# A table of 1,326 steps written anew: the order and the engine of every step of a thresholded attention on one core

## The chip, the cores and the metric

The kernel runs on one core of a Trainium2 chip. The metric is the device time of one execution in microseconds (us), lower is better. Three runs of the kernel before gave 174.76, 174.87 and 173.38 us, with a median of 174.76 us.

## The reference

There are 8 x 12 = 96 heads, each with 512 queries and 512 keys of 64 numbers. The weights are a softmax, those not above the threshold of 0.1 are set to zero, what is left is normalized again, and the values are summed with it:

```python
scores = np.einsum('bhqd,bhkd->bhqk', Q, K) * scale
weights = np.exp(scores - np.max(scores, axis=-1, keepdims=True))
weights = weights / (np.sum(weights, axis=-1, keepdims=True) + 1e-10)
weights = np.where(weights > threshold, weights, 0)
weights = weights / (np.sum(weights, axis=-1, keepdims=True) + 1e-10)
return np.einsum('bhqk,bhkd->bhqd', weights, V).astype(np.float32)
```

With 512 random keys very few queries have a weight above 0.1. The kernel finds these few rows and fills the rest of the output with zeros.

## The kernel before, in words

Two heads make a pair (48 of them) and two pairs a quad (24). For each quad, numbered 0 to 23, the steps are these, named as in the plan. SP issues the loads of queries and keys (step `q`, line 334, 512 KB; step `k`, line 330, four transfers of 128 KB). `qcast` (lines 367, 369, 371) turns queries to half precision on ACT, DVE or GpSimd (POOL in the profile). `ktr` (L381) and `qtr` (L410) transpose keys and queries on TensorE (PE), `kev` (L389 on ACT, L391 on DVE) and `qev` (L416) copy the results to SBUF, and `kh` (L396, L398, L400) casts the keys. `sc` (L438) makes the scores of 128 keys for both heads of a pair, `ex` their approximate exponentials (L447 on ACT, L449 on DVE; 384 instructions, two for each `sc`), and `sm` (L468) adds them up on PE into one PSUM bank for a whole group of pairs. `bits` (L425 on GpSimd, L427 on ACT, L429 on DVE) and `norms` (L478) make squared norms for a check that closes the kernel. `z` (L607, SP) fills the output of a quad with zeros, 512 KB each.

The pairs form three groups of 24, 16 and 8. When the last `sm` of a group is done, `y`, `d`, `fl`, `mx` (L486 or L488, L495, L500, L504) find its candidates. They are worked on in six stages x = 0 to 5, three for the first group, two for the second, one for the third. A stage is a chain: `m`, `ix`, `qi` and `qf` (L513, L519, L524, L529) make row numbers; `gq` (L534) gathers query rows with an indirect transfer issued by GpSimd; `xm` and `xev` (L541; L547 on ACT, L549 on DVE) transpose them; `xqk` (L556, PE) makes exact scores; `xexp` (L562, ACT), `xcut` and `xkeep` (L566, L570, DVE) keep what is above the threshold; `vi` and `oi` (L575, L580) turn it into row numbers; `gv` (L585) gathers the value rows and `scatter` (L600) writes them to the output, both indirect transfers issued by GpSimd. So GpSimd issues 18 indirect transfers, and `scatter` of a stage waits for the landing of its `gv`. At the end `nm` and four `check` steps (L491, L750 to L763) feed a branch (L772 to L784) that is not taken.

All loads, keys, casts and squares share 32 buffers of one ring called big; the transposed keys of a quad stay in it until the `xqk` of its stage has read them. A load waits until the step that had the buffer before is done.

No scheduler runs when the kernel is built. `ORDER` (L13) is a string of 1,326 words, a step number in base 36 and a letter for the engine (P PE, V DVE, A ACT, G GpSimd, S the SP queue, Q the queue of ACT, N none). `Plan.order` walks through it, takes buffers and emits the step; each engine works its own steps in that order, one after the other:

```python
        for i, e in seq:
            name, engs, _, deps, _, fn, takes, gives, _ = self.ops[i]
            assert e in engs and all(self.ids[d] in done for d in deps), name
            for pool, key in takes:
                self.held[pool, key] = idle[pool].pop(0)
            fn(e)
            for pool, key in gives:
                idle[pool].append(self.held[pool, key])
            done.add(i)
```

Only steps with more than one engine in their list can change engine: `qcast`, `kev`, `kh`, `ex`, `bits`, `y` and `xev`, and the loads of quad 0, which may go by SP or by ACT's queue. The loads of quads 0 and 1 are cut into halves of 128 KB (keys of one head) and 256 KB (queries of one pair); these are the first twelve transfers.

Of the kernel before, what the change touches and what calls it, by code (L numbers as in the profile page):

```python
# [853 lines left out]
```

## Time and profile before

| | kernel before |
|---|---|
| median of three runs | 174.76 us |
| the profiled execution | 173.97 us |
| its span in the trace | 172.1 us |
| busy: PE, DVE, ACT, GpSimd | 159.3, 150.6, 146.7, 133.7 us |
| exponentials on ACT and on DVE | 238 and 146 |
| zero fills, key loads, query loads by SP | 24, 95, 26 transfers |

The table says that four engines are busy for most of the span, so it does not tell what bounds the time. The rows are read for three stretches: the ramp (to 16 us), the steady part (16 to 149.5 us, where the last exponential ends), and the tail, where the last group's chain runs.

### The profile page before, as it was taken

How to read it: one execution, taken by the hardware profiler on the slowest of the kernel's cores; microseconds unless marked ns; L12 is line 12 of the kernel's file. 1: busy time of each engine (PE TensorE's matmuls, PEld its weight loads, DVE VectorE, ACT ScalarE, POOL GpSimd, SP SyncE). 2: the span in 40 equal slices, each digit the busy share in tenths (PEclk: the TensorE clock that was granted, in tenths of full speed). 3: DMA queues.
4: the chain of work that ended last, by engine and by line, in shares of the span. 5: the costliest groups of instructions: out<-in, count | busy, mean ns of one | idle time of the engine just before them, and what ended most of it. 6: DMA issues, size and time to landing. Idle time of an engine off the chain costs nothing.

```text
span 172.1 us, 5805 instructions
## 1 busy us (share of the span) xinstructions
PE 159.3 (93%) x2190; PEld 62.5 (36%) x2190; DVE 150.6 (88%) x353; ACT 146.7 (85%) x294; POOL 133.7 (78%) x201
## 2 busy tenths in 40 slices
PE   5699999999999999999989999989999999999940
PEld 1253544342444234334432443434324333432410
DVE  5398999899999989989999899999999999989630
ACT  2279999999999999999899999999999999746300
POOL 5049794999988979993796999999899985226762
PEclk9999999999999999999999999999999999999996
DMA  4999998959899999878999996999999980000000
GB/s 103 290 281 175 268 255 224 265 132 313 183 244 304 277 229 339 242 181 251 276 280 289 221 272 156 365 409 311 318 304 338 415 344 13 2 3 8 3 3 9
DMA packets 67453, 38.27 MB, mean 222 GB/s; under 512 B 51941, under 2 KB 64349, under 8 KB 67424
## 3 DMA queue, kind: packets, MB, share of 16 engines
...
q0 software_dynamic: 576, 0.13, 0.5%
q10 hardware_dynamic: 528, 0.13, 0.3%
...
## 4 chain that ended last, share of the span: by engine, by line
PE 55%; DMA 15%; DVE 10%; POOL 6%; ACT 4%; issue 4%; SPq 2%; POOLq 0%; DVEq 0%
PE one L438 20%; PE sum L468 19%; DMA qs<-in_Q_dram,idx 7%; PE one L556 6%; PE one L381 4%; PE one L410 3%; ACT e L447 3%; DMA out_dram<-zero 3%; POOL big L425 2%; DMA big<-in_K_dram 2%; DVE e L449 2%; DMA big<-in_Q_dram 2%; POOL qh L371 2%; PE one L541 2%; SPq L330 2%
## 5 line engine op out<-in xcount | busy, mean ns | idle before, releaser
L447 ACT ACTIVATE e<-one 128x512 f16<-128x512 f32 x238 | 123.3, 638 | 3.0 <-PE one L438 2.5
L449 DVE TENSOR_SCALAR e<-one 128x512 uint16<-128x512 f32 x146 | 93.5, 682 | 4.2 <-PE one L438 3.4
L438 PE MATMUL one<-big 64*128 64x512 f16 x384 | 66.4, 385 | 0.3
L468 PE MATMUL sum<-e,w_s 128*32 128x512 f16 (+1 forms) x768 | 58.4, 385 | 0.3 <-DVE y L495 0.2
L425 POOL TENSOR_TENSOR big<-big 128x512 bf16<-128x512 f16 x56 | 56.9, 1037 | 0.0
L400 POOL CAST big<-big 128x512 f16<-128x512 f32 x46 | 27.6, 611 | 8.6 <-DVE big L429 3.3
L371 POOL CAST qh<-big 128x512 f16<-128x512 f32 x45 | 26.5, 612 | 7.9 <-DVE qh L369 6.3
L438 PEld LDWEIGHTS <-big 64*128 64x128 f16 x384 | 17.1, 95 | 36.5 <-issue 28.0
L468 PEld LDWEIGHTS <-w_s 128*32 128x32 f16 (+1 forms) x768 | 15.3, 95 | 31.6 <-issue 27.0
L389 ACT COPY big<-one 128x512 f32<-128x512 f32 (+1 forms) x33 | 18.5, 591 | 3.8 <-PE one L381 3.8
L416 DVE COPY big<-one 128x512 f16<-128x512 f16 (+1 forms) x52 | 19.2, 396 | 1.2 <-PE one L410 0.7
L381 PE MATMUL one<-identity_f,big 64*128 64x64 f32 x384 | 18.1, 231 | 1.6 <-DMA big<-in_K_dram 1.4
L381 PEld LDWEIGHTS one<-identity_f,big 64*128 64x128 f32 x384 | 16.5, 143 | 6.4 <-issue 2.7
L534 POOL DMA_INDIRECT qs<-in_Q_dram,idx x6 | 6.4, 1072 | 12.5 <-DVE idx L524 12.2
L391 DVE COPY big<-one 128x512 f32<-128x512 f32 (+1 forms) x19 | 12.5, 657 | 1.3 <-PE one L381 0.6
L556 PE MATMUL one<-big,xq 128*32 128x512 f32 x96 | 11.5, 598 | 0.4 <-DVE xq L549 0.2
L410 PE MATMUL one<-identity_h,qh 64*128 64x64 f16 x384 | 10.8, 193 | 0.7 <-DVE qh L369 0.4
L410 PEld LDWEIGHTS <-qh 64*128 64x128 f16 x384 | 8.7, 96 | 7.2 <-issue 3.1
L600 POOL DMA_INDIRECT out_dram<-vr,idx x6 | 6.4, 1065 | 2.6 <-issue 1.1
L585 POOL DMA_INDIRECT vr<-in_V_dram,idx x6 | 6.4, 1060 | 2.3 <-DVE cut L566 1.2
L562 ACT ACTIVATE one<-one 128x512 f32<-128x512 f32 x6 | 3.5, 584 | 5.4 <-PE one L556 5.3
L429 DVE TENSOR_SCALAR big<-big 128x512 int32<-128x512 int32 x15 | 7.3, 491 | 0.1
...
## 6 DMA issues: line engine op xcount, KB each, us to landing
...
qs<-in_Q_dram,idx POOLq DMA_INDIRECT x6, 3.4
vr<-in_V_dram,idx POOLq DMA_INDIRECT x6, 2.4
out_dram<-vr,idx POOLq DMA_INDIRECT x6, 2.2
```

Source lines behind the costliest of these rows:

```text
L371: behind(nc.gpsimd.tensor_copy(dst, src))
L381: nc.tensor.matmul(dst[i][:, c:c + D], lhsT=src[ps, n0 + n, r, :], rhs=identity_f32[ps, ps], is_transpose=True, start=True, stop=True)
L389: nc.scalar.copy(dst, src)
L400: behind(nc.gpsimd.tensor_copy(dst, src))
L410: nc.tensor.matmul(dst[i][:, c:c + D], lhsT=src[ps, n0 + n, r, :], rhs=identity_h[ps, ps], is_transpose=True, start=True, stop=True)
L416: nc.vector.tensor_copy(qk_b[big("qk", q)][:, 0, n0:n0 + k, i * SO * D:(i + 1) * SO * D], src)
L425: behind(nc.gpsimd.tensor_tensor(out=dst[:, n, :], in0=src[:, n, :], in1=src[:, n, :], op=ALU.mult))
L438: nc.tensor.matmul(one[at("one", ("sc", hp, t, h))][:], lhsT=qk[ps, 1, n, t * P:(t + 1) * P], rhs=qk[ps, 0, n, :], start=True, stop=True)
L447: nc.scalar.activation(dst, src, ACTF.Exp, scale=scale, bias=-11.0 * math.log(2.0))
L449: nc.vector.tensor_scalar(dst.bitcast(u16), src, scale * LOG2E * 1024.0, 4096.0, op0=ALU.mult, op1=ALU.add)
L468: nc.tensor.matmul(dst[32 * j:32 * j + 32, :], lhsT=w, rhs=x, start=first, stop=False, skip_group_check=True)
L556: nc.tensor.matmul(one[at("one", ("xs", x))][sl, :], lhsT=xq_b[at("xq", x)][:, n, sl], rhs=kt_b[big("kt", quads[j])][:, n, :], start=(n == ...
```

## The change

Only the string is changed. The steps, their instructions and the six stages are the same.

```diff
@@ -10,7 +10,7 @@
-ORDER = """6N fS 1G gS 7P hS 8P 5V 18S 24S 9P 22S aP 23S bP 16S 17Q 2vS iV jP 2tS nP kV lA cP mA
...
+ORDER = """6N fS gQ 1G hS 18Q 7P 24S 22S 8P 3G 5V 23S 16Q 9P 17S aP jP 2tS bP kA lV 2uS iG mA 2vS
...
```

Steps that change engine, as counts of the two tables: `ex` on ACT 238 before, 232 now, on DVE 146 and 152; `kev` on ACT 33 and 35, on DVE 19 and 17 (those of whole quads on ACT 27 and 31, those of halves 6 and 4); `bits` on ACT 5 and 10, on DVE 15 and 11, on GpSimd 28 and 27; `kh` on ACT 1 and 2; `qcast` on DVE 3 and 0, on ACT 0 and 1, on GpSimd 45 and 47; `y` on ACT 1 and 2.

The end of GpSimd's work, in the order in which it stands, before. The index tile tells the stage: idx_174 to idx_179 are stages 0 to 5.

```order
L534 DMA qs_183<-in_Q_dram,idx_177 128x64
L534 DMA qs_184<-in_Q_dram,idx_178 128x64
L534 DMA qs_185<-in_Q_dram,idx_179 128x64
L600 DMA out_dram<-vr_196,idx_176 49152x64
L585 DMA vr_197<-in_V_dram,idx_177 128x64
L600 DMA out_dram<-vr_195,idx_175 49152x64
L600 DMA out_dram<-vr_197,idx_177 49152x64
L585 DMA vr_198<-in_V_dram,idx_178 128x64
L585 DMA vr_199<-in_V_dram,idx_179 128x64
L600 DMA out_dram<-vr_198,idx_178 49152x64
L600 DMA out_dram<-vr_199,idx_179 49152x64
```

And now, from the last squares (L425) on:

```order
L425 TENSOR_TENSOR big_137<-big_133 128x512 x4
L600 DMA out_dram<-vr_194,idx_175 49152x64
L534 DMA qs_183<-in_Q_dram,idx_177 128x64
L600 DMA out_dram<-vr_196,idx_176 49152x64
L534 DMA qs_184<-in_Q_dram,idx_178 128x64
L534 DMA qs_185<-in_Q_dram,idx_179 128x64
L585 DMA vr_197<-in_V_dram,idx_177 128x64
L600 DMA out_dram<-vr_197,idx_177 49152x64
L585 DMA vr_198<-in_V_dram,idx_178 128x64
L585 DMA vr_199<-in_V_dram,idx_179 128x64
L600 DMA out_dram<-vr_198,idx_178 49152x64
L600 DMA out_dram<-vr_199,idx_179 49152x64
```

The stores of stages 1 and 2 (idx_175, idx_176) stood among the transfers of the last three stages; now the one stands ahead of all three `gq` and the other behind the first of them. The `gv` of stages 4 and 5 now follow the store of stage 3 as before, with one store fewer ahead of that.

The end of ACT's work before, from the last exponential on. The cut tiles cut_191 to cut_193 are stages 3 to 5.

```order
L447 ACTIVATE e_150<-one_106 128x512
L486 ACTIVATE y_162<-sum_113,small 64x512
L547 COPY xq_187<-one_108 128x256
L562 ACTIVATE one_110,cut_191<-one_110 128x512
L427 ACTIVATE big_130<-big_122 128x1024
L427 ACTIVATE big_129<-big_127 128x1024
L562 ACTIVATE one_111,cut_192<-one_111 128x512
L547 COPY xq_187<-one_108 128x256
L562 ACTIVATE one_112,cut_193<-one_112 128x512
L427 ACTIVATE big_144<-big_125 128x1024
```

And now, from `y` on:

```order
L486 ACTIVATE y_162<-sum_113,small 64x512
L547 COPY xq_187<-one_109 128x256
L562 ACTIVATE one_111,cut_191<-one_111 128x512
L547 COPY xq_186<-one_107 128x256
L427 ACTIVATE big_133<-big_134 128x1024
L427 ACTIVATE big_125<-big_142 128x1024
L427 ACTIVATE big_133<-big_134 128x1024
L562 ACTIVATE one_109,cut_192<-one_109 128x512
L427 ACTIVATE big_122<-big_120 128x1024
L562 ACTIVATE one_111,cut_193<-one_111 128x512
L427 ACTIVATE big_119<-big_141 128x1024
L427 ACTIVATE big_122<-big_120 128x1024
```

Six squares (L427) stand behind `y` now, against three: three between the copy of stage 4 (L547, xq_186) and its exponential (cut_192), one between that and the exponential of stage 5 (cut_193), two at the end. A seventh, not in these rows, stands just ahead of `y` and behind the last exponential of the steady part; three more stand earlier, against two. The copy of stage 5 has moved from ACT to DVE, that of stage 4 from DVE to ACT.

The first loads in SP's queue before. big_114 and big_115 hold keys and queries of quad 0, big_117 and big_116 those of quad 1, big_120 is the query load of quad 2.

```order
L330 DMA big_114<-in_K_dram 128x4x64 x2
L334 DMA big_115<-in_Q_dram 128x2x256 x2
L334 DMA big_116<-in_Q_dram 128x2x256
L330 DMA big_117<-in_K_dram 128x4x64 x2
L330 DMA big_114<-in_K_dram 128x4x64
L334 DMA big_116<-in_Q_dram 128x2x256
L330 DMA big_117<-in_K_dram 128x4x64 x2
L334 DMA big_120<-in_Q_dram 128x4x256
```

And now:

```order
L330 DMA big_114<-in_K_dram 128x4x64
L334 DMA big_115<-in_Q_dram 128x2x256
L334 DMA big_116<-in_Q_dram 128x2x256
L330 DMA big_117<-in_K_dram 128x4x64 x2
L330 DMA big_114<-in_K_dram 128x4x64
L330 DMA big_117<-in_K_dram 128x4x64 x2
L334 DMA big_116<-in_Q_dram 128x2x256
L334 DMA big_120<-in_Q_dram 128x4x256
```

SP issues one half of the first keys and then the first queries. The other half of the first keys now goes out on ACT's queue at the same time, and behind it on that queue the other queries and one more key half of quad 0 (before, ACT's queue had one key half of the second pair only).

The loads of later quads change places as well. The one the prediction speaks of is the key load of quad 17. Before, its buffer came from a `qcast` step, and 43 exponentials stand in the table between the load and `ktr` of that quad. Now its buffer is that of the keys released by `xqk` of stage 0, and 14 stand between.

## Rows read from the trace of the kernel before

**Rows 1.** Windows of two stretches: us, busy of each engine, granted clock, DMA share, GB/s.

```profile
6.00:16.00 10.00, 9.31 (x106) 4.28 (x106) 7.91 (x21) 7.60 (x17) 5.01 (x11) 1.00 1.11 253
16.00:149.50 133.50, 131.74 (x1908) 51.80 (x1912) 127.65 (x248) 131.48 (x265) 115.67 (x171) 1.00 0.91 259
```

**Rows 2.** Instruction groups by shape: count, busy us, mean ns, idle before.

```profile
L447 ACT ACTIVATE e<-one 128x512 f16<-128x512 f32 x238 | 123.3, 638 | 3.0 <-PE one L438 2.5
...
L371 POOL CAST qh<-big 128x512 f16<-128x512 f32 x45 | 26.5, 612 | 7.9 <-DVE qh L369 6.3 <-DVE y L500 0.7 <-DMA big<-in_Q_dram 0.6
...
L389 ACT COPY big<-one 128x512 f32<-128x512 f32 x27 | 16.4, 637 | 0.0
...
L427 ACT ACTIVATE big<-big 128x1024 bf16<-128x1024 f16 x5 | 5.2, 1053 | 0.0
...
L369 DVE CAST qh<-big 128x512 f16<-128x512 f32 x3 | 1.3, 420 | 2.3 <-DMA big<-in_Q_dram 2.3
...
L396 ACT CAST big<-big 128x512 f16<-128x512 f32 x1 | 0.6, 617 | 0.4 <-DVE big L391 0.4
```

**Rows 3.** Chain that ended last, 158 us to the end: start, us, what.

```profile
162.33 0.21 DVE idx L575
...
163.00 2.42 DMA vr<-in_V_dram,idx
```

**Rows 4.** Timeline of GpSimd, 148 to 170 us: start, us, instruction, idle before.

```profile
148.24 1.07 POOL L534 DMA_INDIRECT qs<-in_Q_dram,idx  x1 [3.75 <-DVE idx L524]
151.31 0.99 POOL L534 DMA_INDIRECT qs<-in_Q_dram,idx  x1 [2.01 <-DVE idx L524]
...
159.84 1.28 POOL L600 DMA_INDIRECT out_dram<-vr,idx  x1 [0.31 <-issue]
161.69 1.01 POOL L600 DMA_INDIRECT out_dram<-vr,idx  x1 [0.57 <-DVE cut L566]
163.00 1.05 POOL L585 DMA_INDIRECT vr<-in_V_dram,idx  x1 [0.30 <-DVE ix L529]
164.36 1.02 POOL L585 DMA_INDIRECT vr<-in_V_dram,idx  x1 [0.31 <-issue]
166.26 1.01 POOL L600 DMA_INDIRECT out_dram<-vr,idx  x1 [0.88 <-DVE okm L763]
167.62 1.00 POOL L600 DMA_INDIRECT out_dram<-vr,idx  x1 [0.35 <-issue]
```

**Rows 5.** Timeline of ACT, 148 to 162.5 us.

```profile
150.51 0.68 ACT L486 ACTIVATE y<-sum,small 64x512 f32<-64x512 f32 x1 [1.02 <-PE sum L468]
...
154.41 1.99 ACT L427 ACTIVATE big<-big 128x1024 bf16<-128x1024 f16 x2
157.41 0.58 ACT L562 ACTIVATE one<-one 128x512 f32<-128x512 f32 x1 [1.01 <-PE one L556]
...
160.56 0.58 ACT L562 ACTIVATE one<-one 128x512 f32<-128x512 f32 x1 [2.04 <-PE one L556]
```

**Rows 6.** Chain that ended last, first 8 us.

```profile
1.47 0.88 SPq L330
...
2.40 3.50 DMA big<-in_Q_dram
```

**Rows 7.** Timeline of ACT, first 9 us.

```profile
6.03 0.37 ACT L389 COPY big<-one 128x256 f32<-128x256 f32 x1 [3.32 <-PE one L381]
```

**Rows 8.** Line 330 (key loads), issues of 0.7 to 1.45 us.

```profile
DMA to landing us min/median/max: 2.8/3.0/3.3
```

**Rows 9.** Timeline of PE, 76 to 103.5 us.

```profile
89.89 1.92 PE L556 MATMUL one<-big,xq 128*32 128x512 f32 x16
...
98.71 0.65 PE L381 MATMUL one<-identity_f,big 64*128 64x64 f32 x16
```

**Rows 10.** Line 330, the four key loads issued from 92.3 us.

```profile
L330 SPq DMA_DIRECT2D big<-in_K_dram x4: 546/606/1116, 92.4 to 94.8; - x4
...
DMA to landing us min/median/max: 3.8/4.4/4.4
```

More of the change, by code (lines that the diff above doesn't have):

```diff
@@ new lines @@
+ORDER = """6N fS gQ 1G hS 18Q 7P 24S 22S 8P 3G 5V 23S 16Q 9P 17S aP jP 2tS bP kA lV 2uS iG mA 2vS nP cP oV 3qS pV qP 3pS 12P sA rV yP dP 10A zV 26P 13A 25G 27V 1aP 28A 1bA 29V 0G 2aP uP 1cV 19A eP 2bV wA 52S 2cV 1eP 14V 2wG vA 2hP 1fV 1dG tP 2jA 11P 1gV 31P 2iA 1xG 2xP 32V 1tP 2yV 2zA 2lP 33V 30A 1pP 1vV xP 1qA 1uV 38P 2mA 3rG 3aV 1hP 1rA 53S 3sG 1wP 39V 1jA 3gP 1yG 6fS 15P 1iA 2nV 34P 3iA 3hV 2dP 36A 3cP 2fV 2eA 3tP 3kG 3dV 35A 6gS 2oP 3uA 3vV 1lP 2pP 7sS 1zN 1mA 1nV 3yP 3eA 3wG 3zV 56P 2qA 40V 3xG 57A 58V 45P 41P 46A 47V 1oP 54G 49P 42A 2rV 1kP 55G 4bA 2gP 43V 4lP 4aA 59G 95S 5bP 4nA 37P 3lG 5cV 1sP 4mA 4dP 5dV 4tP 4eA 4fV 6jP 4vA 4uV 5qP 6kA 3bP 5aG 3mN 5sV 2kP 6lA 5mP 6hG 5uP 5rA 5nV 5eP 6iG 7tS 5oA 4gP 5wV 4cP 5fA 6mG 5iP 96S 5gV 6oP 5vA 6nG aiS 4oP 6pV 5kA 4pP 6qV 7wP 5jA 7nV 6vP 7xA 7yV 5lP 7oG 5xP 4rA 44P 6xV 5yP 6wA d8S 5tP 60V 5zA 7fP 6zP 4qA 7hV 5hP 3jP 7gA 70V 7jP 99P 7kA 71V 77P 9aA 5pP 7uG 78V 7iP 79A 6yP 7vG 7lV 66P 9bA 7zG 81P 67A 7bP 82V 68A 3fP 97G 6rP 83V 7dA 98G ajS 2sP 7cV 6sA 88P 80G 8cP bwS 6tV 89A 7mP 9cG 9eP bvS 8eV 8aA 73P 9dG 8dA 7eP 7pN 9fV amP 4xG 75A 9gV 74V a5P anA 8kP a7V aoA 4wP 69P 8mA d9S 7aP 8lV 62P apG a6A 84P fzS 64V 8gP 86A 76P elS 85V 72P 8hA 48P 4hP 8iA 63V 9lP 4jA a8P akG 9mV 87P 9nA 9pP alG 4iV 8sP 9rA 8fP 6aG 8tV 8oP 9qA arP 8pA 65P asV a9P 8uA atV 8nP aaV 8qA auP 4yG 9hP awA abV b6P emS avA 4kP 9jV 61P 4sP 9iA fyS b7V b2P b8A dcP bxG 4zN b3V b4A acP byG ddA a1P deV bzP a2A aqG a3V 9xP 9oP daG c0V c1A ayP 9yA 8bP b0V 9zA a4P c2G biP 9tP azV 6bG bkA c4P 9sP c5V bjA axP 9vV 8vP hbS 9uA 8wP baP c6V 8xA 8jP 8yV dfG 6cN cfP bcA epP bbV dgG cgA cbP chV eqA dbG beP cdA 8rP ccV c3G 9kP bgA dhP bfV adG cjP erA 9wP hcS diV ckA cvP clV czP 21S cxA 8zP djV ciP d0A ioS ceP d1V esG ecP cwA bmP g0G edV dkP eeA bhP etG bdP boA bnV b9P dmA enG crP dlV doP ctA cmP k1S eoG csV e4P dqA cnP dpV e5A b1P 6uP efP coA e6V euP cpA dsP bqV e8P evV dtA cyP g1G e9V drP duA blP g2P ewV eaA brV exP g3A g4V fdP bsN aeG bpP ffA cuP ezV ipS f5P feA flP lfS f7V f6A cqP dnP k2S ebP eyV fmA g5G afN g7P fnA f1P g8V f9P hdG f2A dvP g9V e7P heG faA f3V c7P giP g6G fbA c9V foP a0P gjA 90G f0P gkV c8A fhP hfP fiV fjA isP hgV hhA b5P itA leS 91G iuV dwP gaP dxA gqP gcV fcP gbA f8P f4P grV dyA d2P h2P gsV iqG 92N geP h3A fpP ekS h4V ivG dzP ggA fgP gdP 51S irG frV gfA gtP gmP fqV hiG hkP goA guP k3G hlV ghP gwA fsP hmV glP hjG gnA e0P gvV gyP 2G e2A hnP gzV gpP e1A gxP h0V caP hpA ixP hzP hoA iyV lgG i7P i1A h1P izV h5P k4G e3P i8A i9V fkP lhG i0A qvS hvP xtV j4P iwG hwA 20P tlS 7qP xuV j5A 4G btP 3nP msS hxA k5P xvN xwV piS j6A j8P xxV 50P k6A mrS agP 93P k7A xyV jcP j9A xzP 6dP y0V jeA ydV i3P xrV y2G jdA hqP i2P y1V i5A jaV ibP 3oS ifP i4A jfP k8G igV o5S joP idA hyP ijG icV ihA yeP hrP jqA yfV iiP ygV htA hsV kaP liP jpA kbV jgP yhG ikV ljA iaP kcV ilN jkP lkA jhV khP jiA huP egG jmV y3P kiA kjA jlV jsP j0P h6A y4V klP j1V kkP y5P k9G ehA j2V ysV kmA jtV eiN juA jwV ktP knA o4S mtG yiP kuV y6A d3G kpP yjV h7A l1P kvV ykP y7V l2V krA h8N l3A y8V phS llG kqA lnP lmG ylA kxP loV mvP muG kzA ymV lpV ieP d4G kyA ynV ksP jnP mwA uxS m2P mxV meP m4A m6P m3V l4P mgA koP pjG n0P d5N mfV m7A lyP m8A myG jrP n1V o8P m0V lzA o6G s8S kdP n2V o9A o7G maP quS kfV j7P oaA mzG jvP mcV keA n7P jxG n3P mbA n8V m1P m5P n4A l0P n5V ytP n9A nbP plP s7S yuV ncV ndA lqP obG jyN pmA lsV nnP mmG pnA mdP n6P yvV lrV noA nvP l5P npA nxV odP 7rS l6A neP oeV m9P ocG l7A 6eS nwV luP miP pkG lwA d7S ofV nqP j3P mjV mkA qwG ogP mqS pqP lvA ohV poG nrP 94S oiA mhP qxG prV naP nsA tkS osP psV ywG ooP ntA otV jbP ltP opA kgP oqV ptP ouA mnG qyP yoV puV pvA q1P qzA l8P q2V orP q3A lxP r0V ldS p0P owP ppG p1A okP moN y9V p2V pwP oyA s9G mlP i6P omV uyS olA saG p8P qdP oxV paA sbP nzG qfA p9V nfP buS scA ozP ngV onP qeA ojP sdV qlP nhA q5P r1G k0S yxP qmV q6A r2G q7V r3P yyA p4P seG qnA r4V nuP haS p5A ftG q9P r5V pxP qbA qaV jjP p3P pzA q8P pyV riP p6A njP rkV sgP rjA yqG nyP shV nkA qgP ryP siV nlA r6P srP tmG rzA yzP ssV r8A ybG stV r7A s0V p7P yaV z0A ovP fuV waS reP ypV fvN tfV rqP rgA toP z1V rfV sfG rrA pbP z2V uzG r9P rsA qoP tnG rmP tpV tqA t3P s6S roA q4P t5V ttP trG t4A o3S nmP tuV tsG rnA qhP ahS ruP tvV qjA v0G niP rwV pgS u4P qiA ycG twP z3V u5V rvA kwP q0P rpP txA u6V t7P o0G tyA raP t9V uoP t8A rlP uqV qcP rbA v1P rcA upV u8P v2A usG rtP o1N z4V v3V sjP tjS u9A szP skV wbS uaA rdP rxP t0A t1V fxS snP u0P slA v4G s1P spV inS rhP u2A qkP utG u1V uwS v6P z7A svP v7V weP swA z8V wfA ugP v8V z9N smP wgA sxV v5G u3P suP soA z5G uhV ucP vtP uiA tzP ueV t6P udA w1P zaV vuA vxP sqP vzA ufP w2V wcG ujP vyA taP vvV whG v9P w9S qtS w3A vpP wiG vbV vaA vdP u7P wdG vrV vfA vwP ubP s2G vqA zbV wjP ukP veA vsP wkV uuN umA vlP ulV vhP vmA vgP wlV w0P vjA vnV s3G tbP wuP viA tdV unP voP wwA t2P wvV tcA wmP xmS x2P zcV woA x6P yrG s4N vcP x4A x8V w4P urP x3A wxP wnV wyP x7A wqP x0V zdP wzA x5P syP zeV wrA vkP pcV xeP wsA zgG xaP xgV teP xfA wpP x9P xcV xbA x1P xhP pdA zrV wtP z6G w5V xdP zsP 106A peN zhP ztV 107V d6P ziA ejP zvG zjP 108N 109V 10aV 10bV zuV 10cP zkA 10dV zwP zlV 10fG zmV jzP zxA s5P l9A zyP znV zfV zoV xiA zpG laA 10gP pfP 10hV zzA lbN 10iP qpA 100V 101V zqG 103V tgV 102V imP thN fwP 10jA xnP 104G o2P w6A uvP 10kV 10lV lcP tiP h9P qqA w7N w8P 10mV 10eV 10sV xjV 10oG 10nV xkN qrN 10rV xlP mpP qsP xoP xsV xpP xqP 105G 10qV 10tV 10pG"""
```

1 line of the change is left out of this document (removed).

## The prediction

> **What bounds the kernel now.** I read the busy time by stretch first [rows 1]. From 16 to 149.5 us, where the last exponential ends, ACT is busy 131.48 of 133.50 us, DVE 127.65, GpSimd 115.67. PE shows 131.74, but matmuls are pipelined, so that number is no proof that PE is full. ACT with 2.02 us of idle time is the fullest engine: work added to it there costs time, work taken from it gains. DVE has 5.85 us free. From 6 to 16 us ACT is busy 7.60 of 10.00 us and DVE 7.91: the ramp is short of data, and ACT can take up to 2.40 us more there without a loss. What the reader is to see is that a share of "busy" over the whole span hides this: the engines are full in one stretch and half idle at both ends.
>
> Behind 149.5 us the last group's chain counts, and there the timeline of GpSimd [rows 4] and the chain of waits [rows 3] say what ends last. The last stage's `vi` ends at 162.33 + 0.21 = 162.54. Its `gv` starts at 164.36, 1.8 us later, since three transfers stand ahead of it on GpSimd: a store of stage 1 at 159.84, the store of stage 3 at 161.69, and `gv` of stage 4 at 163.00. Two that follow each other start 1.31 to 1.36 us apart (161.69, 163.00, 164.36; 166.26 and 167.62): about 1 us of issue and 0.3 us of idle. From `gv` of stage 4 to its landing it takes 2.42 us [rows 3], and the store starts at 166.26, 0.84 us behind the landing at 165.42. The last store's 167.62 is both 3.26 us behind its own `gv` (2.42 + 0.84) and 1.36 behind the store ahead of it.
>
> **The tail.** The new order takes the stores of stages 1 and 2 away from this place. They go to where GpSimd waits: it is idle 3.75 us ahead of 148.24 and 2.01 us ahead of 151.31 [rows 4], and one store of 1.3 us goes into each gap. So they should cost nothing. If that cover were gone, each would put 1.3 us on `gq` of stage 4. Without the old store, `gv` of stage 3, its store, and `gv` of stage 4 should all be issued before `vi` of stage 5 ends; the last `gv` then starts 0.3 us behind 162.54, at 162.84, and the last store at 162.84 + 3.26 = 166.10 instead of 167.62: a gain of 1.5 us. It can't be more, unless the chain to `vi` gets shorter, and that chain is the same list of steps. It can be less, down to nothing, if `vi` is late by 1.5 us. ACT is where this could come from. It now has six squares behind `y` instead of three; two of them took 1.99 us [rows 5]. Three stand between the copy and the exponential of stage 4, about 3 us, where the exponential of stage 4 had to wait until 157.41 anyway behind 1.01 us of idle time. I expect it about 0.9 us late, at 158.3: the first exponential and its readout end near 154.5, the copy of stage 4 cannot start before its transpose, near 155, and three squares follow. That delays stage 4 only. One square then follows, to 160.1, and the exponential of stage 5 at 160.56 had 2.04 us of idle time ahead of it, so it starts on time, with less than half a microsecond to spare. The square ahead of `y` lies in the 1.02 us that ACT waits there at 150.51, so it costs 0 to 0.1 us. The closing check reads the last `norms`; fewer squares on DVE and more on ACT keep that about where it was, and it is not on the chain in these rows.
>
> **The steady part.** ACT loses 6 exponentials at 123.3 / 238 = 0.518 us (busy time by count, since neighbours overlap) [rows 2], 3.11 us. It gains 4 key copies of whole quads at 16.4 / 27 = 0.607 us, 2.43 us, and loses two of halves at 0.37 us [rows 7], 0.74 us. Up to its last exponential it gains one square at 1.05 us, one `y` at 0.68 us [rows 5], one `kh` at 0.62 us, and one `qcast` that no row shows on ACT; the nearest is that `kh`, same shape, 0.62 us [rows 2]. The sum is +1.55 us. Of it the half copies, `kh` and `qcast` (+0.50) are work for quads 0 and 1 in the ramp, where ACT has 2.40 us idle [rows 1]: I count nothing. The rest, +1.05, falls on the full stretch. Bounds: all of it is paid, +1.05, or the new order also removes ACT's 2.02 us of idle time, -1.0. I take +0.5, the middle between paid in full and absorbed, since one profile cannot say how well another order packs. DVE gets 6 exponentials more and loses two whole key copies net, some squares and three casts; it stays near where it was and has room.
>
> **The ramp.** The first transposition needs both key halves, and before, the second one was issued at 1.47 and the queries at 2.40, landing 3.50 us later [rows 6]. Issued together at 0.74, two key halves on two queues landed 2.8 and 3.3 us later [rows 8], by 4.1; before, the first key copy could start only at 6.03, after 3.32 us of idle time [rows 7]. So keys come over 1 us sooner, and then the queries set the start. They are issued 0.93 us sooner, at 1.47, and cast on GpSimd in 0.61 instead of on DVE in 0.42 us [rows 2]: a gain of up to 0.74. But the other queries now go out on ACT's queue at the same moment. The two halves sharing the engines cost the later one 0.5 us in rows 8, and the queries are twice as large, so the whole gain may go, leaving the longer cast, +0.2. I take -0.4. The rows show queues sharing. The Trainium skill, "DMA: Bandwidth & Descriptors", "Issuing engines are not separate DMA queues", is sterner: transfers from different engines run on the same 16 DMA engines and interleave, and a second issuing engine saves only issue time. By that rule the two query halves would land together and I would count 0 here, and the sum below would be 0.4 us higher; the 2.8 against 3.3 us agree with interleaving at least in part.
>
> **The sum.** -1.5 (tail) + 0.5 (steady) - 0.4 (ramp) = -1.4 us. The profiled execution took 173.97 us (span 172.1 and 1.87 around it), which makes 172.6 us; it stood 0.45% below the median of the runs shown, so against 174.76 this is 173.3 us, 0.8% faster. About 1%, 1.75 us, is what a measurement can tell from no change.
>
> **Rivals.** First, the whole order packs better: ACT's idle time in the steady part goes, -1.0 instead of +0.5. That is 171.1 us, or 171.8 against the median. For it speaks that 2.02 us of idle time on ACT and 5.85 on DVE are there; against it that ACT's work grows, and that 98.5% is already full. Chance 0.22.
>
> Second, the tail's gain is taken back: the squares on ACT start late and hold up the exponential of stage 5, which has under half a microsecond to spare. If `vi` of stage 5 is 1.5 us late the last `gv` stands where it stood: 174.1, or 174.9. Against it: each step of that chain still finds its engine idle in rows 5. Chance 0.13.
>
> Third, slower: the key load of quad 17. It now waits for `xqk` of stage 0, which ends at 89.89 + 1.92 = 91.81, and its `ktr` started at 98.71, 6.9 us later [rows 9]; two more PE steps stand between now. Four key loads issued over 2.4 us with the last landing after 3.8 to 4.4 us take 6.2 to 6.8 us [rows 10]. So they land just in time if the queue holds as much as it did then. Each 512 KB more ahead of them costs 2.0 us at the 259 GB/s of this stretch [rows 1]. PE works in order, so a late `ktr` stops scores and sums, and ACT and DVE run dry behind it. Two such transfers, a query load and a zero fill, make 4.0 us less the 0.1 us of slack: 172.6 + 3.9 = 176.5, or 177.3. It decides from some 3.2 us of delay on, where the forecast's gain is used up and 1% is lost on top. Against it: these transfers have older buffers and may be through by then. Chance 0.13.
>
> **How the numbers follow.** The forecast has 0.52, with its own range from 172.4 to 174.3 for the bounds of ramp and steady part; about a third of that lies under 173.0, where faster by over 1% begins. Faster: 0.18 + 0.22 = 0.40. Within 1%: 0.34 + 0.13 = 0.47. Slower: 0.13. The range from 171.4 to 175.6 takes in the second rival, most of the first, and leaves the slower one out.
>
> **What would show it.** On GpSimd's timeline the last `gv` should start within 0.5 us of its `vi`, and the last store 3.3 us later; from the start of ACT's last `y` to the end of the span it should take 1.5 us less than before. ACT's first key copy should start near 5 us instead of 6.03, and the last exponential should end within 1 us of 149.5. The forecast is wrong if that end moves by more than 1.5 us, if `ktr` of quad 17 shows PE waiting for a key load, or if the last exponential of the tail waits for squares on ACT.

## The result, and the profile after

The changed kernel takes 173.18 us (median of 20 runs, 171.97 to 174.11), the kernel before, run beside it, 174.76 us. The ratio is 0.9916, with a 95% interval from 0.9892 to 0.9939: faster by 0.6 to 1.1%. Ratios leave out the runs that are over 1.5% longer than the fastest of their kernel, of which every kernel can have some. The forecast was 173.3. The profiled execution took 172.14 us with a span of 170.4 us; before it was 173.97 and 172.1.

The windows of the two stretches of [rows 1], in the changed kernel (us, then busy time of PE, PEld, DVE, ACT, GpSimd, then granted clock, DMA share and GB/s):

```profile
6.00:16.00 10.00, 9.64 (x105) 3.44 (x106) 8.33 (x21) 8.44 (x19) 6.63 (x9) 1.00 1.21 240
16.00:149.50 133.50, 131.62 (x1904) 52.13 (x1906) 127.56 (x248) 130.73 (x263) 112.04 (x167) 1.00 0.91 259
```

ACT and DVE do more in the ramp (8.44 us against 7.60, 8.33 against 7.91). In the steady part ACT has 2.77 us idle instead of 2.02.

The start, on ACT and its queue (start, us, instruction, what ended the idle time before it), to be laid beside [rows 7]:

```profile
0.75 0.66 ACTq L330 DMA_DIRECT2D big<-in_K_dram  x1
1.45 0.80 ACTq L334 DMA_DIRECT2D big<-in_Q_dram  x1
2.29 0.55 ACTq L330 DMA_DIRECT2D big<-in_K_dram  x1
2.87 1.28 ACT L389 ACT_TABLE_LOAD   x1 [2.87 <-issue]
4.91 0.37 ACT L389 COPY big<-one 128x256 f32<-128x256 f32 x1 [0.76 <-PE one L381]
```

The first key copy starts at 4.91 instead of 6.03, as forecast ("near 5").

The last exponential of ACT ends at 149.62 (149.49 before). The rows of the last eight, in the kernel before and in the changed one:

```profile
145.39 4.10 ACT L447 ACTIVATE e<-one 128x512 f16<-128x512 f32 x8
```

```profile
145.60 4.02 ACT L447 ACTIVATE e<-one 128x512 f16<-128x512 f32 x8
```

The tail on ACT, beside [rows 5] (neighbours overlap, so the square ahead of `y` starts at 149.42):

```profile
149.42 1.14 ACT L427 ACTIVATE big<-big 128x1024 bf16<-128x1024 f16 x1
151.08 0.68 ACT L486 ACTIVATE y<-sum,small 64x512 f32<-64x512 f32 x1 [0.53 <-PE one L519]
...
155.60 2.95 ACT L427 ACTIVATE big<-big 128x1024 bf16<-128x1024 f16 x3
158.46 0.58 ACT L562 ACTIVATE one<-one 128x512 f32<-128x512 f32 x1
...
160.93 0.58 ACT L562 ACTIVATE one<-one 128x512 f32<-128x512 f32 x1 [0.83 <-PE one L556]
```

The exponential of stage 4 comes at 158.46 (forecast 158.3). That of stage 5, at 160.93, still waits for PE and not for a square. The tail on GpSimd, beside [rows 4]:

```profile
149.53 1.06 POOL L600 DMA_INDIRECT out_dram<-vr,idx  x1 [0.31 <-issue]
...
156.54 1.00 POOL L585 DMA_INDIRECT vr<-in_V_dram,idx  x1 [0.30 <-DVE idx L580]
159.65 1.00 POOL L600 DMA_INDIRECT out_dram<-vr,idx  x1 [2.11 <-DVE cut L566]
161.29 1.03 POOL L585 DMA_INDIRECT vr<-in_V_dram,idx  x1 [0.64 <-DVE idx L575]
163.19 1.14 POOL L585 DMA_INDIRECT vr<-in_V_dram,idx  x1 [0.87 <-DVE oks L758]
164.63 1.01 POOL L600 DMA_INDIRECT out_dram<-vr,idx  x1 [0.30 <-issue]
166.43 0.99 POOL L600 DMA_INDIRECT out_dram<-vr,idx  x1 [0.79 <-issue]
```

and the last index on DVE, which answers to [rows 3]:

```profile
162.71 0.21 DVE idx L575
```

The index ends at 162.92 and the last `gv` starts 0.27 us behind it (1.82 before); the last store follows 3.24 us later (3.26 before). So the wait that the forecast wanted to remove is gone, to a tenth of a microsecond.

PE shows no wait at `ktr` of quad 17, 7.5 us behind the end of the `xqk` that frees its buffer (`xqk` at 90.09 with 1.89 us, [rows 9]):

```profile
99.48 0.71 PE L381 MATMUL one<-identity_f,big 64*128 64x64 f32 x16
```

Between the two profiles, `y` starts 0.57 us later (151.08, 150.51) and from there to the end of the span it takes 19.3 us instead of 21.6. The forecast was that this stretch gets 1.5 us shorter. It got 2.3 shorter, and the stretch ahead of it gave part back.

### The profile page after: what moved, and what is told of

It reads as the page before. It is cut to its first block, busy times and chain, and to the rows that moved or that the text cites. A ratio compares the mean times of both kernels' runs of the same rounds, so it can differ in the third digit from the quotient of the medians.

```text
span 170.4 us, 5820 instructions
## 1 busy us (share of the span) xinstructions
PE 159.7 (94%) x2190; PEld 62.4 (37%) x2190; DVE 150.3 (88%) x349; ACT 151.5 (89%) x298; POOL 132.2 (78%) x200
## 4 chain that ended last, share of the span: by engine, by line
PE 69%; SPq 13%; DMA 7%; issue 3%; DVE 3%; ACT 2%; POOL 1%; ACTq 0%; POOLq 0%; DVEq 0%
PE sum L468 25%; PE one L438 25%; SPq L330 11%; PE one L556 5%; PE one L381 5%; DMA big<-in_K_dram 4%; PE one L410 3%; DMA big<-in_Q_dram 3%; SPq L334 2%; PE one L541 2%; PE one L478 2%; PE one L519 1%; POOL out_dram L600 1%; ACT e L447 1%; DVE junk L570 0%
## 5 line engine op out<-in xcount | busy, mean ns | idle before, releaser
L447 ACT ACTIVATE e<-one 128x512 f16<-128x512 f32 x232 | 119.6, 648 | 2.3 <-PE one L438 2.0
L449 DVE TENSOR_SCALAR e<-one 128x512 uint16<-128x512 f32 x152 | 97.0, 683 | 3.1 <-PE one L438 2.0
L438 PE MATMUL one<-big 64*128 64x512 f16 x384 | 67.2, 384 | 0.9 <-issue 0.3
L425 POOL TENSOR_TENSOR big<-big 128x512 bf16<-128x512 f16 x54 | 54.8, 1041 | 2.9 <-DVE big L429 2.8
L371 POOL CAST qh<-big 128x512 f16<-128x512 f32 x47 | 28.1, 616 | 14.4 <-PE one L438 5.1
L400 POOL CAST big<-big 128x512 f16<-128x512 f32 x45 | 27.1, 615 | 2.7 <-DVE cut L566 1.3
L389 ACT COPY big<-one 128x512 f32<-128x512 f32 (+1 forms) x35 | 19.7, 600 | 1.3 <-PE one L381 1.2
L381 PEld LDWEIGHTS one<-identity_f,big 64*128 64x128 f32 x384 | 15.8, 140 | 6.7 <-POOL mask_x L225 1.6
L391 DVE COPY big<-one 128x512 f32<-128x512 f32 (+1 forms) x17 | 10.5, 624 | 2.4 <-PE one L381 1.7
L427 ACT ACTIVATE big<-big 128x1024 bf16<-128x1024 f16 x10 | 10.2, 1059 | 0.0
```

What stands on the lines that cost most here:

```text
L371: behind(nc.gpsimd.tensor_copy(dst, src))
L381: nc.tensor.matmul(dst[i][:, c:c + D], lhsT=src[ps, n0 + n, r, :], rhs=identity_f32[ps, ps], is_transpose=True, start=True, stop=True)
L389: nc.scalar.copy(dst, src)
L400: behind(nc.gpsimd.tensor_copy(dst, src))
L425: behind(nc.gpsimd.tensor_tensor(out=dst[:, n, :], in0=src[:, n, :], in1=src[:, n, :], op=ALU.mult))
L438: nc.tensor.matmul(one[at("one", ("sc", hp, t, h))][:], lhsT=qk[ps, 1, n, t * P:(t + 1) * P], rhs=qk[ps, 0, n, :], start=True, stop=True)
```

## Two chains end this kernel

One more row of each kernel explains most of what follows. It is the flag that closes the norms' check (L776 on DVE), in the kernel before:

```profile
166.83 0.14 DVE L776 TENSOR_SCALAR over_i<-ok 1x1 int32<-1x1 f32 x1
```

and in the changed kernel:

```profile
166.62 0.14 DVE L776 TENSOR_SCALAR over_i<-ok 1x1 int32<-1x1 f32 x1
```

Each engine loads that flag and branches on it, so the end waits for it too. Its chain is: the last squares, PE's last norm sums (L478), the maximum (L491), the flag. In the table below, nine kernels have the span's end 3.69 to 3.77 us behind the flag, while the last store stands anywhere from 3.81 to 5.17 us ahead of it: there the flag set the end. In the other four (before, e11, e12, e13) the flag was ready 5.2 us or more ahead, and the end came 4.25 to 4.65 us behind the last store. The end is the later of the two. The steps behind the branch (L849) agree: there SP waits for the last store for 1.9 us in the kernel before and 0.3 us in the changed one (us in total, times, longest us),

```profile
SPq L849 <- DMA out_dram<-vr,idx: 1.9, 1, 1.9
```

```profile
SPq L849 <- DMA out_dram<-vr,idx: 0.3, 1, 0.3
```

for 2.3, 2.7 and 1.7 us in e11, e12 and e13, and for 0.5 and 0.4 us in e4 and e5; the others have no such row. So in the changed kernel, e4 and e5 the two chains end within a few tenths of a microsecond of each other. The page's chain of waits runs back from the last counted instruction, mostly the last store, and so shows one of the two only.

All times in the table are read from the profiles: the start of ACT's last `y` (L486) is zero, g3 and g5 are the `gv` of stages 3 and 5, "flag" is L776. "By the tail" is 1 + (y to end - 21.55) / 174.76: the ratio that would come out if nothing but the stretch behind `y` had changed. The measured ratio is to the kernel before on the same chip. e2 is not in the table, since its profiled execution was among its longest.

| kernel | g3 | g5 | flag | store to end | flag to end | y to end | by the tail | measured |
|---|---|---|---|---|---|---|---|---|
| before | 7.88 | 13.85 | 16.32 | 4.44 | 5.23 | 21.55 | 1 | 1 |
| changed | 5.46 | 12.11 | 15.54 | 3.94 | 3.75 | 19.28 | 0.987 | 0.9916 (0.9892 to 0.9939) |
| e1 | 7.70 | 13.69 | 17.31 | 4.10 | 3.70 | 21.01 | 0.997 | 0.9985 (0.9951 to 1.0019) |
| e3 | 6.78 | 13.13 | 16.97 | 4.28 | 3.75 | 20.72 | 0.995 | 0.9959 (0.9922 to 0.9995) |
| e4 | 5.45 | 12.18 | 15.61 | 3.81 | 3.77 | 19.38 | 0.988 | 0.9885 (0.9834 to 0.9936) |
| e5 | 5.46 | 12.25 | 15.68 | 3.87 | 3.75 | 19.43 | 0.988 | 0.9904 (0.9864 to 0.9945) |
| e7 | 7.22 | 13.63 | 18.05 | 4.88 | 3.70 | 21.75 | 1.001 | 1.0051 (1.0007 to 1.0094) |
| e8 | 5.48 | 12.71 | 17.40 | 5.16 | 3.69 | 21.09 | 0.997 | 0.9999 (0.9961 to 1.0037) |
| e9 | 7.63 | 13.88 | 17.90 | 4.60 | 3.69 | 21.59 | 1.000 | 1.0014 (0.9972 to 1.0055) |
| e10 | 5.47 | 12.11 | 16.88 | 5.17 | 3.70 | 20.58 | 0.994 | 0.9963 (0.9914 to 1.0011) |
| e11 | 5.46 | 12.18 | 14.26 | 4.44 | 5.58 | 19.84 | 0.990 | 0.9900 (0.9845 to 0.9954) |
| e12 | 7.63 | 13.42 | 14.84 | 4.25 | 6.11 | 20.95 | 0.997 | 0.9975 (0.9924 to 1.0026) |
| e13 | 5.45 | 12.06 | 14.85 | 4.65 | 5.27 | 20.12 | 0.992 | 0.9965 (0.9925 to 1.0005) |

For ten of the twelve kernels the stretch behind `y` alone gives a ratio inside the measured interval; the changed kernel and e13 are 0.8 us slower than it says. A profile is one execution, so differences of some tenths of a microsecond in a row say little.

The time from the last store to the end is not a constant of its own. In the four kernels where the store came last it landed 2.6 to 3.0 us behind its start (2.80 in the kernel before, 2.96 in e13), in the ten other profiles (e2's with them) 2.14 to 2.18 (2.15 in the changed kernel). In those four, and in no other, packets of the instruction queue (8 KB each) start before the store's last packet is through: at 168.60 against 169.54 us in the kernel before, at 168.50 against 168.21 in the changed one. That the one causes the other is not shown.

## The experiments

The edits are given by step names as the plan has them, with the stage (of `bits`: quad and half) behind.

**The stores alone (e1), and the stores put back (e3).** On GpSimd, e1 against the kernel before, and e3 against the changed one:

```diff
 e1
-... last squares, gq 3, gq 4, gq 5, scatter 2, gv 3, scatter 1, scatter 3, gv 4, gv 5
+... last squares, scatter 1, gq 3, scatter 2, gq 4, gq 5, gv 3, scatter 3, gv 4, gv 5
 e3
-... last squares, scatter 1, gq 3, scatter 2, gq 4, gq 5, gv 3, scatter 3, gv 4, gv 5
+... last squares, gq 3, gq 4, gq 5, scatter 2, gv 3, scatter 1, scatter 3, gv 4, gv 5
```

> The kernel before with one edit of its table: the output stores of stages 1 and 2 stand on GpSimd where the changed kernel has them (stage 1's behind GpSimd's last squares, stage 2's behind the query gather of stage 3). Loads, engines and all other steps are as before. Theory 'the tail gain is the stores alone': the last gather starts within 0.4 us of the last index (1.82 us before) and the time falls by 1.2 to 1.8 us, ratio to the kernel before 0.990 to 0.993. Rival 'the gain needs the rest of the new order' (the earlier stores push a query gather or a value gather back, or the last store waits for something else): gather starts earlier, but the last store ends less than 0.5 us sooner, ratio 0.997 to 1.002.

> The changed kernel with the two stores put back among the last gathers of GpSimd as before (stage 2's ahead of the value gather of stage 3, stage 1's behind it). Theory 'the stores alone': the wait between last index and last gather is again 1.5 to 1.8 us (0.27 in the changed kernel), and the time goes back up by 1.2 to 1.8 us: ratio to the kernel before 0.998 to 1.002. Rival 'the rest of the new order makes the gain': less than 0.5 us slower than the changed kernel, ratio 0.991 to 0.995.

Measured: e1 0.9985, e3 0.9959. The theory falls for e1: with the two stores of stages 1 and 2 (the old stores) out of the way, the last `gv` starts 13.69 us behind `y`, 0.16 sooner than before. GpSimd's timeline of e1, from `gv` of stage 3:

```profile
160.53 1.12 POOL L585 DMA_INDIRECT vr<-in_V_dram,idx  x1 [2.54 <-DVE cut L566]
163.87 1.01 POOL L600 DMA_INDIRECT out_dram<-vr,idx  x1 [2.22 <-DVE cut L566]
165.19 1.02 POOL L585 DMA_INDIRECT vr<-in_V_dram,idx  x1 [0.30 <-DVE idx L580]
166.52 1.00 POOL L585 DMA_INDIRECT vr<-in_V_dram,idx  x1 [0.31 <-issue]
```

The store of stage 3 stands 3.34 us behind its `gv`, as the last store stands 3.2 to 3.3 us behind the last `gv`: it waits for that gather's data. And the last two `gv` stand behind it in the same queue, 1.32 and 1.33 us apart. So the last gather starts some 6 us behind `gv` 3, and `gv` 3 waits for its own index on DVE, at 7.70 us behind `y`. In the kernel before this is the same chain: 158.39, 161.69, 163.00, 164.36, 5.97 us. Its first member is not in [rows 4]; the second row here is the wait ahead of the store of stage 3 (ns, then us), which starts at 158.9 and lasts 2.05 us, to the landing of that gather at 160.9:

```profile
158.39 1.14 POOL L585 DMA_INDIRECT vr<-in_V_dram,idx  x1 [1.22 <-DVE cut L566]
```

```profile
L600 POOLq EVENT_SEMAPHORE  x1: 2054/2054/2054, 158.9 to 158.9; - x1
```

The old store at 159.84 only filled the time in which the store of stage 3 waited anyway. In the changed order the two stores do cost: e3's `gv` 3 comes 1.32 us later than the changed kernel's, its last `gv` 1.02 us later, and its median was 174.32 us against 172.95 of e4 on the same chip. Not all of that is the stores' doing: by the table the flag set e3's end, and it was late since DVE's copy of stage 5's queries started 1.72 us behind their first transpose on PE,

```profile
158.20 0.65 PE L541 MATMUL one<-mask_x,qs 128*64 128x256 f32 x4
159.92 0.42 DVE L549 COPY xq<-one 128x256 f32<-128x256 f32 x1 [2.81 <-PE one L541]
```

against 0.69 us in the changed kernel (157.73, 158.42). The transpose itself started 2.5 us behind the gather's issue in both. e3 lies between the two theories: the stores are worth about 1 us on the last `gv` there, and the rest of the new order still gains 0.4%.

**Loads (e2, e4).** e2 is the kernel before with the changed one's first twelve loads, e4 the reverse:

```diff
 e2 (k a.b.h: keys of quad a, pair b, head h; q a.b: queries; [Q]: ACT's queue)
-k 0.0.0, k 0.0.1, q 0.0, q 0.1, q 1.0, k 1.0.0, k 1.0.1, k 0.1.0, k 0.1.1 [Q], q 1.1, k 1.1.0, k 1.1.1
+k 0.0.0, k 0.0.1 [Q], q 0.0, q 0.1 [Q], q 1.0, k 1.0.0, k 1.0.1, k 0.1.0 [Q], k 0.1.1, k 1.1.0, k 1.1.1, q 1.1
 e4
-k 0.0.0, k 0.0.1 [Q], q 0.0, q 0.1 [Q], q 1.0, k 1.0.0, k 1.0.1, k 0.1.0 [Q], k 0.1.1, k 1.1.0, k 1.1.1, q 1.1
+k 0.0.0, k 0.0.1, q 0.0, q 0.1, q 1.0, k 1.0.0, k 1.0.1, k 0.1.0, k 0.1.1 [Q], q 1.1, k 1.1.0, k 1.1.1
```

> The kernel before with the first twelve loads in the changed kernel's order and on its queues, both halves of the first keys at once; all else as before. ScalarE's first key copy should start near 4.9 us (6.03 before). Theory 'ramp carries through': the last exponential ends some 1 us earlier than 149.5 and the time falls by about 0.8 to 1.1 us, ratio 0.993 to 0.996. Rival 'the steady part gives it back' (a stretch further on is bounded by the steps' own order or by another transfer, and not by when the first keys came): first copy early, last exponential within 0.3 us of 149.5, ratio 0.998 to 1.002.

> The changed kernel with its first twelve loads in the order and on the queues of before; all else as changed. First key copy near 6.0 us again. Theory 'the ramp's 1.1 us is used up': since the changed kernel's steady part, with 1.05 us more ScalarE work, ends where it did before, the later start should pass through, the last exponential should end near 150.7 instead of 149.6 and the time should rise by about 1 us: ratio to the kernel before 0.996 to 0.999. Rival 'the steady part does not depend on the first microseconds': last exponential within 0.3 us of 149.6, ratio 0.990 to 0.993.

Measured: e2 0.9946 (0.9907 to 0.9985), e4 0.9885 (six runs). The two disagree. In the old order the new loads seem to gain 0.9 us, as "ramp carries through" has it; in the new order, taking them back costs nothing: the first key copy was 0.71 us later (5.62), the last exponential 0.3 us later, and the time no longer. In e2's profile the first copy stands at 4.99; more is not read from it. What the loads are worth is between nothing and 1 us, and is left open; e2's twelve runs scatter from 172.91 to 178.86 us (median 174.69, the kernel before 175.35).

**TensorE's first microseconds (e9).** A 512-column matmul takes 579 to 634 ns from start to end at first and 372 to 392 ns later. From 10 to 14 us the score matmuls of the changed kernel show the second value,

```profile
L438 PE MATMUL one<-big 64*128 64x512 f16 x12 | 2.5, 377 | 0.1
```

and those of e3, which has the same loads and the same steps up to there, a mean between the two:

```profile
L438 PE MATMUL one<-big 64*128 64x512 f16 x6 | 1.8, 528 | 0.0
```

The step is TensorE's clock. The views print a granted clock of 1.00 (of 2.4 GHz) for both windows, but the kept trace has no record of the clock before 8.55 us in the changed kernel and before 13.37 us in e3; from there to the last microseconds it says 1.00. In all fourteen profiles the last long matmul starts ahead of that first record, and the first short one no more than 0.02 us ahead of it. The level ahead of the record follows from the durations alone: at 1.2 instead of 2.4 GHz 512 columns take 213 ns longer (an estimate), and the scores take 230 ns longer (607 and 377). e9 was made to bring the step forward, by filling the time in which PE waits for the first keys:

```diff
-            lambda e: do_warm(e, "warm", 4), ...
+            lambda e, j=j: do_warm(e, "warm", 12 if j == 4 else 4), ...
```

> The kernel before with eight more of the blank matmuls that TensorE runs while the first keys are on their way (28 instead of 20 ahead of the first transposes); nothing else. In the kernels run so far a 512-column matmul takes 607 ns from start to end in the first microseconds and 377 to 389 ns later, and the step from one to the other comes at 12.2 us in the kernel before and at 9.7 in the changed one; in both TensorE stands idle before the first keys, 1.4 and 0.7 us. Theory 'idle TensorE keeps the matmuls slow, and that is the ramp's gain': without the idle stretch the step comes before 10 us, the scores and sums of the first quads end about 1 us sooner, and the time falls by 0.4 to 1.0 us, ratio 0.994 to 0.998. Rival: the step stands at 12 us or comes sooner without effect, because VectorE and ScalarE set the pace from 8 us on; ratio 0.999 to 1.001.

Measured: 1.0014 (0.9972 to 1.0055); PE's idle time there fell from 1.37 to 0.58 us, and the clock rose at 12.90 us, not before 10. The theory falls. The moment varies by itself: 12.14, 12.56, 11.07, 11.30, 10.51, 9.70 and 10.23 us in the seven profiles that are the kernel before up to there (before, e1, e7, e8, e10, e11, e12); 8.55, 13.37, 11.89 and 11.05 in the four with the changed loads and order (changed, e3, e5, e13). So the profile of the changed kernel had an early one, and its ramp is no measure of what the change does.

**The square ahead of `y` (e5).** The changed kernel with one square moved on ACT:

```diff
-..., last ex, bits 17.1, y, xev 3, xexp 3, ...
+..., last ex, y, xev 3, bits 17.1, xexp 3, ...
```

> The changed kernel with ScalarE's square that stands ahead of y (149.42, 1.14 us) moved behind the copy of stage 3's queries; all else as changed. Theory 'the square holds y': y comes 0.5 us sooner after the last exponential and the time falls by 0.3 to 0.5 us, ratio to the kernel before 0.987 to 0.990 where the changed kernel has 0.9916. Rival 'y waits for TensorE's last sums, as the trace names it': y stands where it did, 1.4 us behind the last exponential, and the square now lies in the path of stage 3's exponential or beside it: ratio 0.991 to 0.995.

Measured: 0.9904 (0.9864 to 0.9945), the changed kernel's within the interval, and `y` stands where it did:

```profile
151.26 0.68 ACT L486 ACTIVATE y<-sum,small 64x512 f32<-64x512 f32 x1 [1.46 <-PE one L519]
```

With the square away, ACT waits 1.46 us for PE instead of 0.53. The rival stands: the square costs nothing, as forecast, and the 0.57 us by which `y` came later are not its doing.

**Stage 3's index early (e7), with the stores (e8).** On DVE, against the kernel before; e8 adds e1's edit:

```diff
-..., qi 5, xev 4, qf 4, bits 17.0, check 1, bits 23.1, xcut 3, xkeep 3, vi 3, oi 3, ...
+..., qi 5, xcut 3, xkeep 3, vi 3, xev 4, qf 4, bits 17.0, check 1, bits 23.1, oi 3, ...
```

> The kernel before with one edit: on VectorE the count, keep and index steps of stage 3 (xcut, xkeep, vi) stand ahead of the copy of stage 4's queries (xev 4), as in the changed kernel, instead of behind it and two squares. GpSimd's order is that of before. Theory 'the last gather hangs on a chain of GpSimd': value gather 3, store 3 behind its data 3.3 us later, then gather 4 and gather 5 at 1.31 and 1.36 us, so that the last gather starts 6.0 us behind gather 3 or 0.3 us behind the last index, whichever is later. Gather 3 would start behind stage 2's store, some 7.0 us after y (7.9 before), the last gather some 13.0 us after y (13.85 before): 0.6 to 0.9 us less, ratio to the kernel before 0.994 to 0.998. Rival, as forecast, 'the old stores are what holds the last gather': nothing gained, 13.8 us after y, ratio 0.999 to 1.001.

> The kernel before with both edits: stage 3's index early on VectorE, and the two old stores early on GpSimd. Theory 'chain of GpSimd': gather 3 starts right behind the last query gather, some 5.7 us after y, the chain would reach the last gather at 11.8, and the last index (12.0 after y) plus 0.3 decides: last gather 12.3 us after y against 13.85, 1.5 us less, ratio 0.989 to 0.993, while either edit alone gives 0.9 us or less. Rival: the later copy of stage 4's queries (0.9 us) moves the last index too, and the gain is under 0.7 us, ratio 0.996 to 1.000.

Measured: e7 1.0051 (1.0007 to 1.0094), e8 0.9999 (0.9961 to 1.0037). In e8 the chain of GpSimd does what the theory says (g3 at 5.48, the last `gv` at 12.71 instead of 13.85), but the time does not follow. The price is the rival's, and it goes further than the index: `xev` 4 is 0.7 us later behind `y` (5.15 in e7, 4.43 before), so PE starts `xqk` 4 late (e7),

```profile
156.68 1.90 PE L556 MATMUL one<-big,xq 128*32 128x512 f32 x13 [0.91 <-DVE xq L549]
```

and everything behind it on PE, the norm sums too. The flag comes 18.05 (e7) and 17.40 us (e8) behind `y` instead of 16.32, and the end stands 3.7 us behind the flag. In e8 it takes the last store 5.16 us to the end, which is to say that the end no longer waits for it.

**The whole tail (e10), and the norm sums taken away (e11, e12, e13).** e10 is the kernel before with e8's edits and the two query copies exchanged:

```diff
 ACT
-..., xexp 3, bits 22.1, bits 14.0, xexp 4, xev 5, xexp 5, ...
+..., xexp 3, xev 4, bits 22.1, bits 14.0, xexp 4, xexp 5, ...
 DVE
-..., qi 5, xev 4, qf 4, bits 17.0, check 1, bits 23.1, xcut 3, xkeep 3, vi 3, oi 3, xcut 4, ...
+..., qi 5, qf 4, xcut 3, xkeep 3, vi 3, bits 17.0, check 1, bits 23.1, oi 3, xev 5, xcut 4, ...
```

e11 is e10, e12 the kernel before and e13 the changed kernel, each with two lines more (e13 with quads 11, 14, 15, 18, 20, 22, 23):

```diff
     def do_norms(eng, q):
+        if q in (10, 13, 14, 15, 17, 18, 19, 22):
+            return
```

> The kernel before with four edits of its tail, all taken from the changed kernel: the two old stores early on GpSimd, stage 3's index early on VectorE, stage 4's query copy (xev 4) on ScalarE instead of VectorE and stage 5's (xev 5) on VectorE instead of ScalarE, so that the early index holds neither. TensorE's order is that of before. Theory 'two chains end the kernel': the stores' chain becomes as short as the changed kernel's (last gather 12.1 to 12.4 us after y, 13.85 before), but the chain of the key norms (TensorE's last norm sums, the maximum, the flag, 3.7 us from the flag to the end) stays as in the kernels with the old order so far, flag 16.3 to 17.9 us after y, and sets the end at 20.0 to 21.6 us after y: ratio to the kernel before 0.992 to 1.000. Rival 'the stores' chain alone sets the end': end 19.5 us after y as in the changed kernel, ratio 0.987 to 0.991.

> The same kernel, and TensorE leaves out eight of its last twelve norm sums (32 matmuls; the norms of eight key quads are then not looked at), so that the flag comes some 2.5 us sooner and the stores' chain alone is left at the end. Theory 'two chains': end at 12.3 + 3.25 + 3.9 = 19.5 us after y, ratio to the kernel before 0.986 to 0.991, clearly below the kernel with all sums. Rival 'stores alone': the same time as the kernel with all sums, within 0.3 us.

> The kernel before with nothing but the same eight norm sums left out. Theory 'two chains, nearly level in the kernel before': its profile has the stores' chain 1.5 us behind the flag's, other profiles with the old tail have the flag last, so without the late sums the end is the stores': 13.85 + 3.26 + 4.2 = 21.3 us after y, ratio 0.996 to 1.000. Rival 'the norm sums set the end of the kernel before': 1 us or more less, ratio below 0.994.

> The changed kernel with seven of its last eleven norm sums left out (28 matmuls; seven key quads are not looked at). In its profile the flag plus 3.75 us and the last store plus 3.94 us fall on the same moment. Theory 'two chains, level in the changed kernel': the flag's goes 1 to 2 us down, the stores' stays, the end comes at most 0.2 us sooner: ratio to the kernel before 0.988 to 0.992, as the changed kernel's 0.9916. Rival 'the flag's chain is the one that is left': 0.5 us or more less, ratio below 0.988.

Measured: e10 0.9963, e11 0.9900, e12 0.9975, e13 0.9965. In e10 the chain of GpSimd is that of the changed kernel (g5 at 12.11 in both), yet the end does not come with it. Its chain of waits ends with the norms (start, us, what):

```profile
164.48 1.60 PE one L478 x12
166.08 0.02 issue
166.10 0.70 DVE nmax L491
...
167.98 0.14 DVE over_i L776
```

The last store had started at 166.51; 3.94 us on, as in the changed kernel, is 170.5, and 4.65, the most where the store set the end, is 171.2. The span ends at 171.7, which is 167.98 + 3.7. In e11, with fewer sums, the flag comes first and the store sets the end:

```profile
166.84 0.98 POOL L602 DMA_INDIRECT out_dram<-vr,idx  x1 [0.91 <-DMA vr<-in_V_dram,idx]
...
165.70 0.14 DVE L778 TENSOR_SCALAR over_i<-ok 1x1 int32<-1x1 f32 x1
```

That is 0.74 us sooner behind `y` than in e10, and 0.6% by the ratios, whose intervals overlap. The four kernels ran on one chip, so they can also be set side by side: the medians of the runs behind the ratios are 174.50 (e10), 173.48 (e11), 174.65 (e12) and 174.21 us (e13). With the sums out of the way the four edits of the tail gain 1.2 us (e11 against e12; 0.6 to 1.8 if these runs are resampled); with the sums in place no gain is clear (e10 against the kernel before: 0.9963, up to 1.0011). The rival "the stores' chain alone" falls by this and by e10's rows. e12 gains nothing that can be measured over the kernel before, as "two chains" expects: the stores stay. e13 is a miss: 0.9965 lies above the ranges of theory and rival (0.988 to 0.992, below 0.988). In it the flag comes 0.7 us sooner behind `y`, the last `gv` stands as in the changed kernel (12.06, 12.11), and yet the end comes 0.84 us later, 4.65 us behind the last store: that store landed 2.96 us behind its start instead of 2.15. In all four profiles in which the flag is written ahead of the last store's start that store landed slower, so the two chains are not quite independent.

## Why the prediction was right, and where it was not

The time was right, and the largest term, the tail, was right in sign and place, but the step that explained it was wrong. That the sum came within 0.1 us of the median is luck: in the two profiles the tail gained 0.8 us more than forecast and the stretch ahead of `y` lost 0.5 us more.

- **"Without the old store ... the last `gv` then starts 0.3 us behind 162.54"**. It does, 0.27 us behind its index, a gain of 1.55 us for a forecast of 1.5. But the prediction gave this to the two stores, and e1 shows that they alone bring 0.16. Three edits together do it (e8, e10): stage 3's index ahead on DVE, so that `gv` 3 starts 5.46 us behind `y` instead of 7.88; the stores out of its way (e3: 6.78); and `xev` 4 and `xev` 5 on each other's engine, so that the early index doesn't hold the last one (in e8 it came 0.4 us late). The prediction read the three transfers ahead of the last `gv` as a queue that is full, and missed that one of them, the store of stage 3, was itself waiting, 3.3 us behind its `gv`; its row names a step of DVE as what ended the wait (L566), not the gather's data.
- **"The closing check ... is not on the chain in these rows"**. True before, and the reason why the flag was left out; but the flag had only 5.23 - 3.7 = 1.5 us to spare. That was just the gain forecast, and in the other profiles with the old order on PE the flag came later still (16.88 to 18.05 us behind `y` where no sum was left out). In e10 this second chain keeps 0.5 to 1.2 us of the stores' gain (171.7 less 171.2 or 170.5). The changed order also brings the flag forward (15.54, and 15.61 and 15.68 in e4 and e5), and there the two chains end about level. The prediction had left the flag about where it was. What moved it can be read on PE, though no run tests it by itself: six of eight filler matmuls (L344, whose result nobody reads) now stand behind the last norm sums (0.94 us from 164.26 on), where before all eight stood ahead of the last of them, and the last norm sum ends 13.25 us behind `y` instead of 14.38.
- **The tail's size**, -1.5, was -2.27 between the profiles. The rest is 0.2 us on the way to the last index and 0.5 us from the last store to the end. That last part is 4.25 to 4.65 us wherever the store sets the end, e13 among them, and 0.65 us of it is the landing of the last store (2.80 before, 2.15), so it is no gain to count on.
- **Ramp, -0.4, and steady part, +0.5**, sum +0.1 up to `y`. In the one pair of profiles the ramp was 1.1 us shorter by its first key copy, out of the bounds given (-0.74 to +0.2), and `y` came 0.57 later, so +1.7 behind the ramp. ACT was busy 0.75 us less in the steady part, where the prediction had put 1.05 us of work on it; the ramp took 0.84 us more (8.44, 7.60). None is a good measure: `y` starts anywhere from 150.5 to 153.3 us in kernels that are nearly the same up to there. What the tail does not explain of the measured ratios is +0.5 us in the mean of the five kernels with the new order ahead of `y` (the changed kernel, e3, e4, e5, e13; 0.1 to 0.8) and +0.3 in the seven with the old one (e1, e7 to e12; 0.0 to 0.7). So the two orders differ there by some +0.2 us, less than either set spreads; this does not contradict the +0.1 and does not test its two halves. No run has the new order ahead of `y` with the old tail.
- **The Trainium skill**, "DMA: Bandwidth & Descriptors", "Issuing engines are not separate DMA queues", says that a second issuing engine saves issue time alone; the prediction took that to make the ramp's term 0. The trace agrees that transfers share: the second queries, issued at 1.45 us on ACT's queue, landed 4.87 us later, where the first ones took 3.50 before [rows 6]. It is near the issue time too: the second key half was issued 0.72 us sooner (0.75, 1.47), and the first key copy stands at 4.91 to 5.05 us in the five profiles with the new loads and at 5.46 to 6.21 in the nine with the old ones, 0.8 us apart in the mean. The 1.1 us of the one pair had some luck in it. What reached the end is the open point of e2 and e4.
- **The range.** The forecast's own range ended at 174.3; its upper bounds add up to -1.5 + 1.05 + 0.2 = -0.25 us, which is 174.5 against the median. Nothing hangs on it.
- **The rivals.** "Packs better": ACT's idle time grew to 2.77 us, so no. "Gain taken back by the squares": no exponential waited for one. "Key load of quad 17 late": PE did not wait for it.
